# First attention of a two-layer network in a fixed TensorE order, with a different division of the PSUM banks

## The chip, the cores and the metric

The kernel runs on one core of one Trainium2 chip. The metric is the device time of one launch in microseconds (us). Its engines are named as in the profile: PE is TensorE's matmul (PEld its weight load), DVE is VectorE, ACT is ScalarE, POOL is GpSimd, SP is SyncE, which issues the DMAs here. PSUM, into which PE writes, has eight banks of 512 fp32 columns on 128 partitions.

## The reference

Two layers over 1024 latent tokens and 256 context tokens of width 1024. The first has windowed attention with 16 query heads on 4 key/value heads, a sink logit for each head and a rotary embedding; the second has a two-dimensional neighbourhood attention. The change concerns the first. Cut to it:

```python
q, k, v, g = _split_a(u @ w_in)                  # u: modulated tokens
q, k = axial rotary of q and k                   # context: without
s_lat = q_block @ k[3 blocks of 128] * scale     # |i - j| <= 128, masked
s_ctx = q_block @ kc[256] * scale
p = softmax([s_lat, s_ctx, sink])
o = p_lat @ v_block + p_ctx @ vc                 # sink has no value
y = (o * silu(g)) @ w_out
h = layer_norm(alpha * h + gate * y)
```

## The kernel before

Matmuls work in a reduced fp32 format, and operands are split into a high part and the rest (`wh`, `wl`; `uAh`, `uAl`), so that a projection takes three matmuls for each of eight pieces of the inner dimension: high times high, rest times high, high times rest (L208 to L210, tile `pj`).

The attention runs over head pairs p = 0 to 7. A pair has 10 blocks b of 128 queries (8 latent, 2 context) and two heads, so 20 steps k; `S_A43` is the score of step 43, that is p = 2, b = 1, the second head. Blocks 1 to 6 see five tiles of 128 keys, blocks 0 and 7 four, the two context blocks two. One step is:

- `qkA`: the scores on PE (L705, L706; latent and context keys, for the high and the low half of the key: `kA0_0`, `kA0_1`), into `S_A`.
- `sm_first`: DVE reads the scores out of PSUM, adds the mask and takes the extremum (L318); POOL places the sink in a further column (L323); ACT takes the exponential and its sum (L325).
- `sm_second`: DVE's reciprocal (L329), and POOL's product with it (L330).
- `sm_transpose`: PE transposes the probabilities, one matmul for each key tile (L337, into `T_A`); ACT copies them as the high part (L341, `pth`), DVE subtracts that from `T_A` for the rest (L343, `ptl`).
- `pvA_fn`: when both heads of a block are split, PE multiplies the values with the high parts and then with the rests (L734, into `pvA`, one bank for two blocks). After each second block ACT and DVE add its halves (L743, L745) and POOL multiplies with the gate path `gA` (L748).

`att_steps` lays these out as rows, one for each step k: the transposes of k, the scores of k + 3, and one half of the values of an earlier block. `merge` mixes the rows with the fill, which is the projection of this pair's gate path and of the next pair's queries: it hands out fill in proportion to the cost of the attention work done so far. Between them stand small dot products (`dot_half`, L600, L618, L619), for which `gh` is loaded at the first.

What `merge` emits is only a program order. A scheduler then decides each engine's order from priorities, which `lift` raises for some instructions, and from its own estimate of when operands are ready.

PSUM before is one pool: two tiles of two banks under the tag "big", which scores and transposes take in turn, and four banks under the tag "one" for projections (`pj`) and values (`pvA`).

## Time and profile before

| | us |
|---|---|
| median of three runs | 1442.06 (1436.31 to 1512.86) |
| profiled execution | 1437.72 |
| its span | 1435.9 |
| PE busy in the span | 1388.1 |
| DVE busy | 983.6 |
| ACT busy | 732.4 |
| POOL busy | 632.1 |

A row of the profile's groups names the line, the engine, the operation, the tiles written and read, shapes and count, then the busy time in us and the mean of one in ns, and the idle time of that engine ahead of these instructions with the instruction that ended it. A row of the waits has the waiting instruction, the one waited for, the total in us, the number of times and the longest. A row of the timeline starts with the start and the duration in us.

### The profile page before, as it was taken

How to read it: one execution, taken by the hardware profiler on the slowest of the kernel's cores; microseconds unless marked ns; L12 is line 12 of the kernel's file. 1: busy time of each engine (PE TensorE's matmuls, PEld its weight loads, DVE VectorE, ACT ScalarE, POOL GpSimd, SP SyncE). 2: the span in 40 equal slices, each digit the busy share in tenths (PEclk: the TensorE clock that was granted, in tenths of full speed). 3: DMA queues.
4: the chain of work that ended last, by engine and by line, in shares of the span. 5: the costliest groups of instructions: out<-in, count | busy, mean ns of one | idle time of the engine just before them, and what ended most of it. 6: DMA issues, size and time to landing. Idle time of an engine off the chain costs nothing. (4 is left out here: it accounts for less than half of the span.)

```text
span 1435.9 us, 25168 instructions
## 1 busy us (share of the span) xinstructions
PE 1388.1 (97%) x8815; PEld 1214.4 (85%) x8816; DVE 983.6 (68%) x2216; ACT 732.4 (51%) x1561; POOL 632.1 (44%) x779
## 2 busy tenths in 40 slices
PE   8999999999999999999999999999999999998995
PEld 5888898888988888788898899888988899887774
DVE  4658887878888788566433765555565565667798
ACT  4337776676776778332222545554455444557210
POOL 0326766667666666233311333333233323336664
PEclk9999999999999999999999999999999999999998
DMA  9472114123222123434287565555555565374453
GB/s 370 167 237 79 51 63 125 52 78 100 71 71 63 56 84 117 134 129 134 74 257 221 147 187 171 138 162 152 160 150 165 137 180 153 101 206 146 116 135 92
DMA packets 117229, 195.05 MB, mean 136 GB/s; under 512 B 9328, under 2 KB 57840, under 8 KB 117104
## 3 DMA queue, kind: packets, MB, share of 16 engines
q1 hardware_dynamic: 117104, 193.45, 44.5%
q8 instruction: 70, 1.15, 0.3%
q14 instruction: 55, 0.45, 0.1%
HBM read 141.51 MB, written 51.90 MB: 135 GB/s over the span
## 5 line engine op out<-in xcount | busy, mean ns | idle before, releaser
L330 POOL TENSOR_SCALAR s_B<-s_B,rs_B 128x640 f32<-128x640 f32 (+1 forms) x128 | 101.4, 793 | 293.4 <-DVE rs_B L329 264.3
L208 PE MATMUL pj<-uBh,wh 128*128 128x512 f32 (+1 forms) x448 | 175.9, 393 | 0.0
L209 PE MATMUL pj<-uBl,wh 128*128 128x512 f32 (+1 forms) x448 | 170.2, 380 | 0.0
L210 PE MATMUL pj<-uBh,wl 128*128 128x512 f32 (+1 forms) x448 | 170.1, 380 | 0.0
L325 ACT ACTIVATE s_B<-s_B,m_B 128x640 f32<-128x640 f32 (+1 forms) x128 | 102.9, 804 | 129.2 <-DVE m_B L318 129.0
L325 ACT ACTIVATE s_A<-s_A,m_A 128x641 f32<-128x641 f32 (+2 forms) x160 | 119.5, 747 | 83.2 <-DVE m_A L318 64.1
L164 POOL TENSOR_TENSOR wl<-wr,wh 128x512 fp32r<-128x512 f32 x64 | 87.0, 1360 | 160.1 <-ACT wh L162 148.1
L330 POOL TENSOR_SCALAR s_A<-s_A,rs_A 128x640 f32<-128x640 f32 (+2 forms) x160 | 129.3, 808 | 62.4 <-DVE rs_A L329 56.3
L318 DVE CUSTOM_DVE_ANT_0 s_A<-S_A,msk,nsk 128x640 f32<-128x640 f32 (+2 forms) x160 | 123.5, 774 | 32.5 <-PE S_A L706 17.0
L343 DVE TENSOR_TENSOR pt_B<-T_B,pt_B 128x640 fp32r<-128x640 f32 (+1 forms) x128 | 100.9, 788 | 62.8 <-ACT pt_B L341 62.4
L208 PE MATMUL pj<-uAh,wh 128*128 128x512 f32 (+1 forms) x384 | 140.1, 365 | 0.8 <-DVE otmp L745 0.8
L209 PE MATMUL pj<-uAl,wh 128*128 128x512 f32 (+1 forms) x384 | 137.6, 358 | 0.0
L210 PE MATMUL pj<-uAh,wl 128*128 128x512 f32 (+1 forms) x384 | 137.3, 357 | 0.0
L343 DVE TENSOR_TENSOR ptl_A<-T_A,pth_A 128x640 fp32r<-128x640 f32 (+2 forms) x160 | 114.1, 713 | 14.1 <-PE pvA L734 7.0
L337 PE MATMUL T_A<-ident,s_A 128*128 128x128 f32 x672 | 100.8, 274 | 10.5 <-DVE m_A L318 5.5
L337 PEld LDWEIGHTS T_A<-ident,s_A 128*128 128x128 f32 x672 | 77.5, 140 | 36.7 <-issue 10.0
L341 ACT CAST pt_B<-T_B 128x640 fp32r<-128x640 f32 (+1 forms) x128 | 84.3, 659 | 47.3 <-PE T_B L337 46.7
L318 DVE CUSTOM_DVE_ANT_0 s_B<-S_B,bias 128x640 f32<-128x640 f32 (+1 forms) x128 | 100.3, 784 | 10.9 <-PE S_B L1038 10.0
L341 ACT CAST pth_A<-T_A 128x640 fp32r<-128x640 f32 (+2 forms) x160 | 96.3, 602 | 15.8 <-PE T_A L337 14.3
L210 PEld LDWEIGHTS pj<-uBh,wl 128*128 128x128 f32 x448 | 84.3, 188 | 16.6
L337 PE MATMUL T_B<-ident,s_B 128*128 128x128 f32 x608 | 88.1, 274 | 6.9 <-POOL gB L1079 2.7
L209 PEld LDWEIGHTS pj<-uBl,wh 128*128 128x128 f32 x448 | 84.7, 189 | 9.1
(219 smaller groups left out, 3879.8 us busy)
## 6 DMA issues: line engine op xcount, KB each, us to landing
kB<-kdB SPq DMA_DIRECT2D x64, 320.0 KB, 5.3
gw<-in_wadaT SPq DMA_DIRECT2D x48, 256.0 KB, 2.8
vdB<-st SPq DMA_DIRECT2D x20, 512.0 KB, 3.4
vB<-vdB SPq DMA_DIRECT2D x16, 640.0 KB, 4.5
wada<-in_wadaC SPq DMA_DIRECT2D x16, 512.0 KB, 9.6
kdB<-st SPq DMA_DIRECT2D x16, 512.0 KB, 2.8
qdB<-st SPq DMA_DIRECT2D x16, 512.0 KB, 3.5
qB<-qdB SPq DMA_DIRECT2D x32, 256.0 KB, 4.6
```

The costliest lines, as they stand in the source:

```text
L164: e.tensor_tensor(lo, r, f32(hi), ALU.subtract)
L208: mm(pt[:, :n], hi[:, sl], rh, start=kt == 0, stop=False)
L209: mm(pt[:, :n], hi[:, sl], rl, start=False, stop=False)
L210: mm(pt[:, :n], lo[:, sl], rh, start=False, stop=kt == KT - 1)
L318: nc.vector.tensor_tensor_reduce(outp, sc, in1, scale, init if init is not None else 3e38, ALU.add, ALU.min, accum_out=s.m)
L325: nc.scalar.activation(s.t[:, :n], s.t[:, :n], AF.Exp, bias=s.m, scale=-1.0, accum_out=s.sum)
L330: nc.gpsimd.tensor_scalar(s.t[:, : s.w], s.t[:, : s.w], s.rs, 1.0, ALU.mult, ALU.mult)
L337: nc.tensor.transpose(tp[:, k * P : (k + 1) * P], s.t[:, src * P : (src + 1) * P], ident)
L341: nc.scalar.copy(pt.hi[:, :n, hl, :], tv)
L343: nc.vector.tensor_tensor(pt.lo[:, :n, hl, :], tv, f32(pt.hi[:, :n, hl, :]), ALU.subtract)
```

## The change

The order of work up to the start of the first attention, and from the output projection on, stays as it was. In between:

- PSUM is divided anew while the first attention runs (`Banks`, pool "psA"): one tile of two banks for scores, one bank each for the first four transposes of the first and of the second head (`T0`, `T1`), one bank for the fifth transposes of both heads (`T2`), one bank for values, two for projections. After the first block of the output projection the old division comes back.
- `sm_transpose` for the first attention: four transposes into T0 or T1, the fifth into T2, where the second head's lies beside the first's. The first four are split for each head, the fifth tiles of both heads together after the second head. That gives 48 instructions more on ACT and on DVE.
- All PE instructions of pairs 0 to 6 are pinned to the program order (`pin`); those of pair 7 are not.
- `merge` has a lead of 1000 and a burst of 600 there: no more than one piece of fill (three projections) between two steps of attention, and one piece ahead.
- Values of blocks with even b stand in one row, both halves; those of odd b remain apart.
- In pairs 2, 4 and 6 the first three scores come about a row later.
- The instructions behind the values (L743, L745) have a priority raised by 60.

In the new kernel all matmuls have the line L94 and the transposes L367; the split is at L371 and L373.

```diff
+        def one(self, name):
+            if name[0] == "T":
+                return self.ps.tile([P, 512], F32, tag=name[:2], bufs=1, name=name)
+            if self.att:
+                return self.ps.tile([P, 512], F32, tag="pv" if name[:2] == "pv" else "pj", bufs=1 if name[:2] == "pv" else 2, name=name)
+            return self.ps.tile([P, 512], F32, tag="one", bufs=4, name=name)
...
-    def merge(att, fill, lead=0.0):
+    def merge(att, fill, lead=0.0, burst=1e9):
...
-            if jf < len(fill) and (ia == len(att) or jf < need or cf - lead <= ca * (tf - lead) / ta):
+            if jf < len(fill) and (ia == len(att) or jf < need or (run < burst and cf - lead <= ca * (tf - lead) / ta)):
...
+        m = min(n, 4)
+        tp = psone(f"T{hl}_{name}")
+        for k in range(m):
+            transpose(tp[:, k * P : (k + 1) * P], order[k])
+        if n == 5:
+            if hl == 0:
+                pt.fifth = psone(f"T2_{name}")
+            transpose(pt.fifth[:, hl * P : (hl + 1) * P], order[4])
+        split(pt.hi[:, :m, hl, :], pt.lo[:, :m, hl, :], tp[:, : m * P].rearrange("p (k q) -> p k q", k=m))
+        if n == 5 and hl == 1:
+            split(pt.hi[:, 4], pt.lo[:, 4], pt.fifth[:, : 2 * P].rearrange("p (h q) -> p h q", h=2))
...
+            def v_both(k=k):
+                pv(k - 3, 0)
+                pv(k - 3, 1)
...
             if split and 0 <= k - 2 < n and last_of_unit(k - 2):
-                row.append((costs[2] / 2, v_first, 0))
+                if subs[k - 2][1] % 2:
+                    row.append((costs[2] / 2, v_first, 0))
             elif split and k - 3 >= 0 and last_of_unit(k - 3):
-                row.append((costs[2] / 2, v_second, need(k - 3, k + ahead)))
+                if subs[k - 3][1] % 2:
+                    row.append((costs[2] / 2, v_second, need(k - 3, k + ahead)))
+                else:
+                    row.append((costs[2], v_both, need(k - 3, k + ahead)))
...
+    pinned.append(True)
     for p in range(8):
-        att = [x for row in rowsA[p * 20 : (p + 1) * 20] for x in row]
+        rows_p = [list(row) for row in rowsA[p * 20 : (p + 1) * 20]]
+        if p == 7:
+            pinned.clear()
+        elif p % 2 == 0 and p:
+            s = [rows_p[n].pop(1) for n in range(3)]
+            rows_p[1].append(s[0])
+            rows_p[2].insert(1, s[1])
+            rows_p[2].append(s[2])
+        att = [x for row in rows_p for x in row]
...
-            merge(att, gprojA(p) + qprojA(p + 1), lead=0.0)
+            merge(att, gprojA(p) + qprojA(p + 1), lead=1000.0, burst=600.0)
```

Three places of the order. First PE in pair 2, from the transposes of step 43 on. In the names `T_A43` is a tile of transposes, `S_A46` one of scores, `pj18_1` a projection; the last number of each name only counts tiles. Before:

```order
L337 MATMUL T_A43_2910<-ident_63,s_A43_2817 128x128 x5
L208 MATMUL pj18_1_2848<-uAh1_106,wh19_2273 128x512
L705 MATMUL S_A46_2927<-kA1_0_2126,qA4_2426 128x384
L706 MATMUL S_A46_2927<-kA1_0_2126,qA4_2426 128x256
L705 MATMUL S_A46_2927<-kA1_1_2682,qA4_2426 128x384
L706 MATMUL S_A46_2927<-kA1_1_2682,qA4_2426 128x256
L209 MATMUL pj18_1_2848<-uAl1_109,wh19_2273 128x512
L210 MATMUL pj18_1_2848<-uAh1_106,wl19_2274 128x512
L734 MATMUL pvA2_0_2942<-pth_A40_2803,vA1_2167 128x256 x4
```

and after:

```order
L367 MATMUL T1_A43_2963<-ident_63,s_A43_2861 128x128 x4
L367 MATMUL T2_A42_2924<-ident_63,s_A43_2861 128x128
L94 MATMUL S_A46_2973<-kA1_0_2167,qA4_2449 128x384
L94 MATMUL S_A46_2973<-kA1_0_2167,qA4_2449 128x256
L94 MATMUL S_A46_2973<-kA1_1_2722,qA4_2449 128x384
L94 MATMUL S_A46_2973<-kA1_1_2722,qA4_2449 128x256
L94 MATMUL pj18_1_2879<-uAh1_106,wh19_2291 128x512
L94 MATMUL pj18_1_2879<-uAl1_109,wh19_2291 128x512
L94 MATMUL pj18_1_2879<-uAh1_106,wl19_2292 128x512
L367 MATMUL T0_A44_2992<-ident_63,s_A44_2900 128x128 x4
L367 MATMUL T2_A44_2997<-ident_63,s_A44_2900 128x128
```

Before, four value matmuls and six projections stood between the transposes of steps 43 and 44 (the last three projections are behind the quoted rows); after, three projections do, and the fifth tiles of step 42 and of step 44 use the same bank.

Then DVE at the same place (`s_A46` is the read of the score, `rs` the reciprocal, `ptl` the split, `otmp` the sum of the values). Before:

```order
L343 TENSOR_TENSOR ptl_A42_2872<-T_A43_2910,pth_A42_2871 128x5x128
L318 ISA s_A46_2932,m_A46_2933<-S_A46_2927,msk_141,nsk_142 128x640
L318 ISA m_A46_2933 128x1
L329 RECIPROCAL rs_A46_2935<-sum_A46_2934 128x1
L318 ISA s_A47_2967,m_A47_2968<-S_A47_2962,msk_141,nsk_142 128x640
```

and after:

```order
L358 RECIPROCAL rs_A45_2936<-sum_A45_2935 128x1
L347 ISA s_A46_2978,m_A46_2979<-S_A46_2973,msk_141,nsk_142 128x640
L347 ISA m_A46_2979 128x1
L373 TENSOR_TENSOR ptl_A42_2918<-T1_A43_2963,pth_A42_2917 128x4x128
L373 TENSOR_TENSOR ptl_A42_2918<-T2_A42_2924,pth_A42_2917 128x256
L358 RECIPROCAL rs_A46_2981<-sum_A46_2980 128x1
L347 ISA s_A47_3006,m_A47_3007<-S_A47_3001,msk_141,nsk_142 128x640
```

The split of step 43 stood ahead of the read of step 46 and stands behind it now, in two instructions.

Last, PE at the start of the attention. Before, fourteen projections of `pj10_0` stand ahead of the first score; these are the last two of them and what follows:

```order
L208 MATMUL pj10_0_1115<-uAh0_105,wh11_991 128x512
L209 MATMUL pj10_0_1115<-uAl0_108,wh11_991 128x512
L705 MATMUL S_A0_1119<-kA0_0_975,qA0_1030 128x256
L706 MATMUL S_A0_1119<-kA0_0_975,qA0_1030 128x256
L705 MATMUL S_A1_1131<-kA0_0_975,qA1_1031 128x256
L706 MATMUL S_A1_1131<-kA0_0_975,qA1_1031 128x256
L210 MATMUL pj10_0_1115<-uAh0_105,wl11_992 128x512
```

and after, from the first projection of `pj10_0` on:

```order
L94 MATMUL pj10_0_1119<-uAh0_105,wh10_989 128x512
L94 MATMUL pj10_0_1119<-uAl0_108,wh10_989 128x512
L94 MATMUL pj10_0_1119<-uAh0_105,wl10_990 128x512
L94 MATMUL S_A0_1123<-kA0_0_979,qA0_1034 128x256 x2
L94 MATMUL S_A0_1123<-kA0_1_982,qA0_1034 128x256 x2
L94 MATMUL pj10_0_1119<-uAh0_105,wh10_989 128x512
L94 MATMUL pj10_0_1119<-uAl0_108,wh10_989 128x512
L94 MATMUL pj10_0_1119<-uAh0_105,wl10_990 128x512
L94 MATMUL S_A1_1138<-kA0_0_979,qA1_1035 128x256 x2
```

Three projections now stand ahead of the first score, and the score takes both halves of the key in one go. On SP the two loads of `gh` move from behind two weight loads to right behind the load of the values; on DVE the product with `gh` (L661, L612 before) moves ahead of the read of S_A1, and the load of the second key half of pairs 2, 4 and 6 moves ahead of a weight load.

66 lines of the change are left out of this document (46 added, 20 removed).

## The prediction

> **What bounds the kernel now.** I read the page first.
>
> ```profile
> span 1435.9 us, 25168 instructions
> ...
> PE 1388.1 (97%) x8815; PEld 1214.4 (85%) x8816; DVE 983.6 (68%) x2216; ACT 732.4 (51%) x1561; POOL 632.1 (44%) x779
> ```
>
> TensorE (PE) is busy for 97% of the span, so the time is its work plus the moments in which it waits. The change touches only the first attention, about 95 to 575 us. Stretches of 72 us inside it (columns: length, then busy us of PE, weight loads, VectorE, ScalarE and GpSimd, the clock, DMA share, GB/s):
>
> ```profile
> 144.00:216.00 72.00, 69.48 (x464) 62.33 (x464) 61.08 (x151) 51.75 (x120) 50.20 (x71) 1.00 0.17 56
> 216.00:288.00 72.00, 68.65 (x445) 60.04 (x443) 58.06 (x143) 48.96 (x114) 48.06 (x71) 1.00 0.30 89
> 288.00:360.00 72.00, 70.08 (x451) 60.70 (x450) 59.48 (x145) 50.80 (x116) 48.21 (x69) 1.00 0.31 92
> 360.00:432.00 72.00, 70.68 (x478) 63.76 (x477) 59.36 (x145) 52.70 (x122) 49.67 (x70) 1.00 0.21 67
> 432.00:504.00 72.00, 70.73 (x463) 62.23 (x462) 57.74 (x142) 49.33 (x113) 45.76 (x68) 1.00 0.20 61
> ```
>
> Over these 360 us PE is recorded idle for 360 - 349.62 = 10.4 us at a full clock (1.00); VectorE is busy for 295.7 us, 82%. PE leads, and VectorE is a close second. The groups by line and shape, for 100 to 520 us, say where PE idles and give the prices of the next part:
>
> ```profile
> L337 PE MATMUL T_A<-ident,s_A 128*128 128x128 f32 x584 | 87.3, 274 | 8.2 <-DVE m_A L318 3.9 <-POOL s_A L330 2.8 <-POOL s_A L323 0.4
> L318 DVE CUSTOM_DVE_ANT_0 s_A<-S_A,msk,nsk 128x640 f32<-128x640 f32 x84 | 74.0, 881 | 22.9 <-POOL s_A L330 10.7 <-PE S_A L706 10.1 <-POOL s_A L323 1.0
> L706 PE MATMUL S_A<-kA,qA 128*128 128x256 f32 x280 | 73.5, 284 | 2.0 <-DVE ptl_A L343 2.0
> ...
> L343 DVE TENSOR_TENSOR ptl_A<-T_A,pth_A 128x640 fp32r<-128x640 f32 x84 | 68.9, 821 | 7.1 <-ACT pth_A L341 3.9 <-PE pvA L734 1.7 <-issue 0.4
> ...
> L705 PE MATMUL S_A<-kA,qA 128*128 128x384 f32 x168 | 57.2, 363 | 0.5 <-DVE ptl_A L343 0.5
> ...
> L618 DVE CUSTOM_DVE_ANT_0 gj<-gw,gh 128x512 f32<-128x512 f32 x48 | 38.4, 801 | 0.8 <-DMA gw<-in_wadaT 0.4
> ...
> L318 DVE CUSTOM_DVE_ANT_0 s_A<-S_A,msk,nsk 128x512 f32<-128x512 f32 x28 | 20.7, 749 | 5.0 <-PE S_A L706 4.4
> ...
> L343 DVE TENSOR_TENSOR ptl_A<-T_A,pth_A 128x512 fp32r<-128x512 f32 x28 | 19.2, 686 | 0.0
> ...
> L705 PE MATMUL S_A<-kA,qA 128*128 128x256 f32 x56 | 16.9, 325 | 1.6 <-DVE ptl_A L343 1.1 <-DMA kA<-kdA 0.6
> ...
> L318 DVE DVE_READ_ACCUMULATOR2_ANT m_A<- 128x1 f32 x140 | 11.5, 82 | 0.0
> L343 DVE TENSOR_TENSOR ptl_A<-T_A,pth_A 128x256 fp32r<-128x256 f32 x25 | 10.5, 420 | 5.2 <-PE pvA L734 5.1
> ...
> L612 DVE SCALAR_TENSOR_TENSOR gh<-gth,gh 128x512 f32<-128x512 f32 x4 | 3.2, 796 | 0.8 <-ACT gth L611 0.5 <-issue 0.3
> L611 ACT ACTIVATE gth<-gh 128x512 f32<-128x512 f32 x4 | 2.5, 630 | 0.8 <-DMA gh<-in_cr 0.8
> ```
>
> PE's recorded idle time is before transposes (8.2 us) and scores (2.0 + 0.5 + 1.6 = 4.1): 12.3 us, nothing before projections. Scores and transposes share two tiles of two banks, so each kind waits until VectorE has read the other; the waits name just that:
>
> ```profile
> PEld T_A L337 <- POOL s_A L330: 9.4, 16, 1.4
> PE T_A L337 <- DVE m_A L318: 5.5, 8, 1.2
> ...
> PEld S_A L705 <- DVE ptl_A L343: 4.1, 11, 1.3
> ```
>
> The records hide part of each wait. In the timeline a 512-column matmul is 0.39 us long, yet the next starts 0.23 after it:
>
> ```profile
> 102.31 0.28 PE L705 MATMUL S_A<-kA,qA 128*128 128x256 f32 x1
> ...
> 102.67 0.28 PE L706 MATMUL S_A<-kA,qA 128*128 128x256 f32 x1
> ...
> 102.78 0.40 PE L210 MATMUL pj<-uAh,wl 128*128 128x512 f32 x1
> ...
> 103.72 0.34 PE L705 MATMUL S_A<-kA,qA 128*128 128x384 f32 x1
> ...
> 104.18 0.28 PE L706 MATMUL S_A<-kA,qA 128*128 128x256 f32 x1
> ...
> 104.30 0.39 PE L208 MATMUL pj<-uAh,wh 128*128 128x512 f32 x1
> ...
> 104.53 0.39 PE L209 MATMUL pj<-uAl,wh 128*128 128x512 f32 x1
> ```
>
> ```profile
> 386.81 0.71 PE L337 MATMUL T_A<-ident,s_A 128*128 128x128 f32 x5
> ...
> 387.28 0.48 PE L208 MATMUL pj<-uAh,wh 128*128 128x512 f32 x1
> ```
>
> So each wait is up to 0.39 - 0.23 = 0.16 us longer than its idle time. The three wait rows alone hold 16 + 8 + 11 = 35 waits; with an estimate of 45, PE loses 12.3 + 45 x 0.16 = 19.5 us to waits in the seven head pairs. By the distances between starts about 0.6 us a pair (my estimate) is in many small ones that no bank explains, and I leave those 4 us. **At most some 15 us can be won.** Prices from these rows: three projections 3 x 0.23 = 0.69 us; a full score takes PE 104.30 - 103.72 = 0.58 and is complete 104.18 + 0.28 - 103.72 = 0.74 after its start; a short one (256 + 256) takes 102.78 - 102.31 = 0.47 and is complete after 0.64; five transposes 387.28 - 386.81 = 0.47.
>
> **The change part by part.** *Scores and transposes in banks of their own.* The waits of one kind for the other go: -15 us, the amount above. If the order brought new waits of the same kind the gain would be smaller; at nothing gained it is 0.
>
> *One bank for both fifth tiles.* Transposes of five tiles now put the fifth in T2, and VectorE empties it only after the second head, as its own instruction behind the score read. T2 is single: the next pair's first fifth transpose waits. In the order this reads T2_A42, S_A46, projections, T0_A44, T2_A44. From the start of S_A46: its score is complete at 0.74; VectorE reads it (0.881 + 0.082), splits T1_A43 (0.686), then T2_A42 (0.420), to 2.81. PE arrives at T2_A44 at 0.58 + 0.69 + 4/5 of 0.47 = 1.65. **It waits 1.16 us.** For the block pair around T2_A48, three projections stand ahead of S_A50 and the split of T1 is done earlier: 0.69 + 0.74 + 0.96 + 0.42 = 2.81 against 0.69 + 0.58 + 0.69 + 0.38 = 2.34, 0.47 us. For T2_A52 the score is short and no projection follows it: 0.69 + 0.64 + 0.83 + 0.42 = 2.58 against 0.69 + 0.47 + 0.38 = 1.54, 1.04 us. For odd blocks a row of values or more stands between, and nothing waits. Sum 2.67 us a pair, and since the order of later pairs is the same, 7 x 2.67 = 18.7 us. If VectorE comes late to the score read (it is busy 82%), up to about 1 us a pair is added; nothing can make it less but a PE that is already late. I take 18.7 and add 2 for lateness, with 17 to 26 as bounds. Here a wait queues everything: S_A47 and all the fill stand behind it on PE.
>
> The Trainium skill (Perfetto Trace Analysis, Matmuls) says that independent matmul groups should rotate through different PSUM banks so that the evacuation of one overlaps the matmuls of the next; by that alone the change would win its 15 us. The same page (Optimization Strategy) says that the same gap repeating can mean that too little PSUM is there for the next tile, which is what a single T2 would show, and by it the sum is the one that I make. No run here has shown T2 yet.
>
> *The two splits more.* VectorE replaces two reads of 640 by two of 512 and one of 256: 2 x (686 - 821) + 420 = +150 ns for each of six pairs of blocks, 0.9 us a head pair, beside PE work; ScalarE does the like. I cost it at nothing beyond T2's chain: VectorE has 18% left. Without that cover it is 7 x 0.9 = 6 us.
>
> *The start.* Before, fourteen projections (from 95.19) stand ahead of the first score; pinned, it is three. Timeline and DMA issues (for 88 to 110 us, the last column is us to landing; then the tile kA over the whole run):
>
> ```profile
> 91.98 2.58 SPq L679 DMA_DIRECT2D kA<-kdA  x4
> ...
> 94.73 0.46 SPq L684 DMA_DIRECT2D vA<-vdA  x1
> ...
> 95.19 0.40 PE L208 MATMUL pj<-uAh,wh 128*128 128x512 f32 x1
> ...
> 98.97 0.91 SPq L609 DMA_DIRECT2D gh<-in_cr  x2
> ```
>
> ```profile
> kA<-kdA SPq DMA_DIRECT2D x6, 320.0 KB, 6.3
> ...
> vA<-vdA SPq DMA_DIRECT2D x1, 640.0 KB, 8.0
> ...
> gh<-in_cr SPq DMA_DIRECT2D x2, 256.0 KB, 5.9
> ```
>
> ```profile
> DMA to landing us min/median/max: 3.9/5.6/8.0
> ```
>
> PE reaches S_A0 at 95.19 + 0.69 = 95.88. Its second half needs the fourth kA load, issued near 93.9, landing near 100.2: PE waits about 4.1 us there (1.7 to 5.8 by the ends 3.9 and 8.0). Before, projections hid this. S_A1 waits for the read of S_A0: 0.3. Then gh: its two loads are now issued right behind vA, near 95.2, and VectorE's product with them stands before the read of S_A1, for which S_A2 waits. By 5.9 us they land at 101.1, by vA's 8.0 at 103.2; I take a value near vA's, the load right ahead in the same queue. From 103.2: tanh 0.63, product 0.80, read 0.83, so 105.5; PE arrives near 102.6, and waits 2.9, or 0.8 by the earlier landing. I take 2.4. Together **6.8 us** (2 to 9).
>
> *Pairs 2, 4, 6.* Their first three scores come a row later, and the second key half is loaded ahead of the weight load that it stood behind. The order leaves about 7 us of PE work between load and use: 5.6 us is hidden, 8.0 is not, 0.7 to 1 each; with a late first transpose I take 2 us for the three (0 to 4).
>
> *No cost:* the one bank of values (its next use is over a row behind the reads that free it), two of projections (a group is 24 matmuls, 5.5 us, behind which the evacuation of the other one lies), values of even blocks in one row (they are read a row later than they are ready). If one of these covers went, a pair would lose some tenths for each group. The last pair is not pinned, and at the hand-over the second gate waits for a copy out of the shared scores tile: 0.5 us. The fill of one piece between steps moves work and adds none.
>
> Sum: -15 + 18.7 + 2 + 6.8 + 2 + 0.5 = **+15 us**. The profiled execution took 1437.72 us (1.8 around its span), the median of the three runs is 1442.06, 4 us above it; against the former the forecast is 1453 us.
>
> **The rivals.**
> *A, the gain holds.* Separate banks take nearly all of 19.5 us and T2 is cheap, since PE is late for another reason when it gets there, and the loads land early (start 2 us): 1437.7 - 19.5 + 2 + some 4 = 1424 us. For it: the waits for the other kind are real. Against: T2's chain consists of rows in a fixed order and PE's work between is counted. Chance 0.12.
>
> *B, about even.* The pinned order is so near to that before that stalls move places: T2 at its low end and the start at 2 us, 1437.7 - 15 + 17 + 2 - 2 = 1440. Chance 0.18. It is also the case in which the change does nothing to speak of.
>
> *C, VectorE becomes the pace.* With a fixed order, PE can't take projections while VectorE is late. VectorE's 82% plus 0.9 us a pair is near 84% of a row's time; where a fill instruction such as the 801 ns product or a rotation stands ahead of a read, each score and split behind it is late and PE pays at once. At 0.3 us for each of 140 rows, 42 us: 1480. It decides against the forecast from an average of 0.1 us a row upward beyond what I counted. For it: 82%, and VectorE's waits for scores (10.1 us on the 640 reads), which show the two in lock step. Against: before, too, VectorE takes its instructions in one order, and the small waits come to 0.6 us a pair. Chance 0.16.
>
> **How the numbers follow.** Forecast case 0.54, at 1453, with 1440 to 1466 from its own bounds (T2 -2 to +5, start -5 to +2, pairs 2, 4 and 6 -2 to +2, gain 12 to 19). A 0.12 at 1424; B 0.18 at 1440; C 0.16 at 1480 (1465 to 1500). The range of 8 in 10 reaches from 1432 (A left out but for its upper edge) to 1472 (the lower part of C): outside lie 0.10 and 0.10. This kernel's runs differ by some per cent, so about 2% (29 us, 1409 and 1466) is what can be told from no change. Faster by more: 0.02, the outermost of A. Slower by more: 0.16, most of C and the edge of the forecast. Same: 0.82.
>
> **What would show it.** In the changed profile: a repeated wait of PE on T2 for ptl_A, three times a pair, 1.1, 0.5 and 1.0 us; hardly any wait of T0, T1 or S for the other kind; PE idle for about 4 us near 96 to 100 us, waiting for DMA of kA, and 2 to 3 us before the third score, by way of gh; from 600 us on nothing but a shift. It is wrong if T2 isn't among PE's waits, if the gap at the start is under 2 us, or if waits stand in all rows rather than in three of ten blocks, which is C.

## The result and the profile after

The change makes the kernel slower: 1491.86 us (median of four runs) against 1440.87. One run of each kernel was slow (1713.88 and 1512.86 us); without these two the ratio is 1.0364, with a 95% interval of 1.0349 to 1.0379. The profiled execution took 1492.0 us. The forecast was 1453 us in a range of 1432 to 1472: the sign was right, the size was wrong by a factor of about 3.5.

First the page, then stretches of the first attention (columns as before: length, busy us of PE, weight loads, VectorE, ScalarE, GpSimd, clock, DMA share, GB/s). The second row is the five stretches of before in one.

```profile
span 1490.2 us, 25208 instructions
...
PE 1398.1 (94%) x8816; PEld 1224.2 (82%) x8816; DVE 985.5 (66%) x2264; ACT 735.5 (49%) x1609; POOL 625.0 (42%) x779
```

```profile
96.00:108.00 12.00, 8.24 (x35) 6.14 (x34) 9.13 (x17) 6.11 (x13) 4.68 (x6) 0.72 1.08 269
144.00:504.00 360.00, 326.57 (x2130) 289.89 (x2129) 280.13 (x711) 237.73 (x575) 219.46 (x324) 1.00 0.23 68
```

PE is recorded idle for 360 - 326.57 = 33.4 us from 144 to 504 us, where it was 10.4. VectorE is less busy there (280.13 us) than before (295.7): it did not become the bound by load. From 96 to 108 us the mean granted clock is 0.72. Now PE's waits:

```profile
PE T_A L367 <- DVE ptl_A L373: 29.1, 22, 1.9
...
PE S_A L94 <- DVE m_A L347: 12.9, 17, 1.6
...
PE yA L94 <- DVE z L983: 8.3, 1, 8.3
...
PE gate L417 <- ACT gates L418: 2.0, 1, 2.0
PE S_A L94 <- DMA kA<-kdA: 1.8, 1, 1.8
PE pj L94 <- DVE st L292: 1.5, 1, 1.5
```

The first row is the fifth tiles' bank T2, 22 waits, three in each pinned pair and one in the last. In the second row a score waits for the read of the score before it. The third is one wait of 8.3 us at the hand-over to the output projection. The prediction had the first with a smaller sum (20.7 us with its 2 for lateness), of the second only what it expected at the start (0.3 us, and 2.4 by way of gh), and the third not at all.

Where the 54.3 us between the two profiled executions lie, by the start of the first score read of each pair and of the first transposes behind the output projection:

| stretch | before | after | more |
|---|---|---|---|
| start to the first score read | 102.7 | 103.4 | 0.7 |
| pairs 0 to 6 | 418.6 | 454.3 | 35.7 |
| last pair and hand-over | 74.0 | 87.7 | 13.7 |
| from there to the end | 840.6 | 844.8 | 4.2 |

The rows come out of these starts, of VectorE's first read in the first and in the last pair and of PE's first transposes of the output block, before:

```profile
102.75 0.75 DVE L318 CUSTOM_DVE_ANT_0 s_A<-S_A,msk,nsk 128x512 f32<-128x512 f32 x1 [2.46 <-PE S_A L706]
...
521.32 0.75 DVE L318 CUSTOM_DVE_ANT_0 s_A<-S_A,msk,nsk 128x512 f32<-128x512 f32 x1
...
595.32 1.09 PE L871 MATMUL uT<-ident,z 128*128 128x128 f32 x8 [1.67 <-ACT z L917]
```

and after:

```profile
103.40 0.75 DVE L347 CUSTOM_DVE_ANT_0 s_A<-S_A,msk,nsk 128x512 f32<-128x512 f32 x1
...
557.66 0.75 DVE L347 CUSTOM_DVE_ANT_0 s_A<-S_A,msk,nsk 128x512 f32<-128x512 f32 x1
...
645.39 1.03 PE L943 MATMUL uT<-ident,z 128*128 128x128 f32 x8
```

One wait on T2 in the timeline, that of T2_A48 in pair 2:

```profile
264.80 0.75 PE L94 MATMUL S_A<-kA,qA 128*128 128x384 f32 x4
...
265.26 0.85 DVE L797 TENSOR_TENSOR otmp<-pvA,otmp 64x256 f32<-64x256 f32 x2 [0.50 <-ACT otmp L795]
...
266.08 0.60 PE L367 MATMUL T_A<-ident,s_A 128*128 128x128 f32 x4
266.14 0.69 DVE L373 TENSOR_TENSOR ptl_A<-T_A,pth_A 128x512 fp32r<-128x512 f32 x1
...
266.75 0.88 DVE L347 CUSTOM_DVE_ANT_0 s_A<-S_A,msk,nsk 128x640 f32<-128x640 f32 x1
...
267.55 0.42 DVE L373 TENSOR_TENSOR ptl_A<-T_A,pth_A 128x256 fp32r<-128x256 f32 x1
...
268.12 0.30 PE L367 MATMUL T_A<-ident,s_A 128*128 128x128 f32 x1 [1.44 <-DVE ptl_A L373]
```

The score is complete near 264.80 + 0.74 = 265.54, but VectorE reads it only from 266.75: the sum of the values (otmp, 0.85) and the first split (0.69) stand ahead. That is 1.2 us that the prediction's chain did not hold.

And the hand-over:

```profile
619.50 1.59 PE L417 MATMUL gate<-ident,dcol 128*128 128x128 f32 x8 [1.96 <-ACT gates L418]
...
630.70 1.28 DVE L983 SCALAR_TENSOR_TENSOR z<-z,yA 128x512 f32<-128x512 f32 x2 [3.37 <-DMA z<-in_htok]
...
632.04 0.80 PE L94 MATMUL yA<-woAh,og 128*128 128x512 f32 x1 [8.34 <-DVE z L983]
632.63 0.63 PE L94 MATMUL yA<-woAl,og 128*128 128x512 f32 x1
633.06 1.06 PE L94 MATMUL yA<-woAh,og 128*128 128x512 f32 x2
```

The second block of the output projection is put into the two projection banks in which the first block's result still stands. VectorE empties them when the residual z has come by DMA, at 630.70, and until 632.04 PE has nothing. Before, the second block had other banks, and PE worked on it while VectorE waited for the same load:

```profile
590.24 1.29 DVE L911 SCALAR_TENSOR_TENSOR z<-z,yA 128x512 f32<-128x512 f32 x2 [3.40 <-DMA z<-in_htok]
590.29 0.39 PE L422 MATMUL yA<-woAh,og 128*128 128x512 f32 x1
```

After, the matmuls behind the gap start 0.43 us apart (632.63, 633.06) in place of 0.23: the granted clock is at 0.50 from 619.9 to 637.0 us.

### The profile page after: what moved, and what is told of

Same layout as the page of the kernel before. It is cut to its first block, busy times and chain, and to the rows that moved or that the text cites. A ratio compares the mean times of both kernels' runs of the same rounds, so it can differ in the third digit from the quotient of the medians.

```text
span 1490.2 us, 25208 instructions
## 1 busy us (share of the span) xinstructions
PE 1398.1 (94%) x8816; PEld 1224.2 (82%) x8816; DVE 985.5 (66%) x2264; ACT 735.5 (49%) x1609; POOL 625.0 (42%) x779
## 5 line engine op out<-in xcount | busy, mean ns | idle before, releaser
L359 POOL TENSOR_SCALAR s_B<-s_B,rs_B 128x640 f32<-128x640 f32 (+1 forms) x128 | 101.8, 796 | 294.0 <-DVE rs_B L358 263.9
L94 PE MATMUL pj<-uBh,wh 128*128 128x512 f32 (+1 forms) x448 | 175.8, 392 | 0.0
L94 PE MATMUL pj<-uBl,wh 128*128 128x512 f32 (+1 forms) x448 | 170.2, 380 | 0.0
L94 PE MATMUL pj<-uBh,wl 128*128 128x512 f32 (+1 forms) x448 | 170.0, 380 | 0.0
L359 POOL TENSOR_SCALAR s_A<-s_A,rs_A 128x640 f32<-128x640 f32 (+2 forms) x160 | 125.6, 786 | 80.3 <-DVE rs_A L358 77.4
L189 POOL TENSOR_TENSOR wl<-wr,wh 128x512 fp32r<-128x512 f32 x64 | 84.0, 1313 | 172.7 <-ACT wh L187 164.7
L94 PE MATMUL pj<-uAh,wh 128*128 128x512 f32 (+1 forms) x384 | 146.1, 380 | 2.3 <-DVE st L292 1.5
L373 DVE TENSOR_TENSOR pt_B<-T_B,pt_B 128x640 fp32r<-128x640 f32 (+1 forms) x128 | 101.0, 789 | 63.9 <-ACT pt_B L371 63.4
L94 PE MATMUL pj<-uAl,wh 128*128 128x512 f32 (+1 forms) x384 | 137.3, 358 | 0.0
L94 PE MATMUL pj<-uAh,wl 128*128 128x512 f32 (+1 forms) x384 | 137.3, 358 | 0.0
L367 PE MATMUL T_A<-ident,s_A 128*128 128x128 f32 x672 | 105.2, 275 | 32.7 <-DVE ptl_A L373 29.1
L94 PE MATMUL S_A<-kA,qA 128*128 128x384 f32 (+1 forms) x576 | 114.2, 316 | 15.0 <-DVE m_A L347 12.9
L367 PEld LDWEIGHTS T_A<-ident,s_A 128*128 128x128 f32 x672 | 81.5, 140 | 52.0 <-issue 25.0
L373 DVE TENSOR_TENSOR ptl_A<-T_A,pth_A 128x512 fp32r<-128x512 f32 (+1 forms) x208 | 117.8, 583 | 9.5 <-ACT pth_A L371 8.3
L94 PEld LDWEIGHTS S_A<-kA,qA 128*128 128x128 f32 x576 | 90.2, 192 | 30.5 <-DVE m_A L347 21.5
L94 PE MATMUL yA<-woAh,og 128*128 128x512 f32 x320 | 103.6, 400 | 8.5 <-DVE z L983 8.3
L371 ACT CAST pt_B<-T_B 128x640 fp32r<-128x640 f32 (+1 forms) x128 | 84.4, 659 | 48.8 <-PE T_B L367 48.3
L371 ACT CAST pth_A<-T_A 128x512 fp32r<-128x512 f32 (+1 forms) x208 | 98.9, 501 | 12.9 <-PE T_A L367 9.5
```

Source lines behind the costliest of these rows:

```text
L94: pin(nc.tensor.matmul(*a, **kw))
L189: e.tensor_tensor(lo, r, f32(hi), ALU.subtract)
L359: nc.gpsimd.tensor_scalar(s.t[:, : s.w], s.t[:, : s.w], s.rs, 1.0, ALU.mult, ALU.mult)
L367: pin(nc.tensor.transpose(out, s.t[:, src * P : (src + 1) * P], ident))
L371: nc.scalar.copy(hi, src)
L373: nc.vector.tensor_tensor(lo, src, f32(hi), ALU.subtract)
```

## The experiments

All but the last are one run each; the kernel before took 1438.0 to 1441.0 us beside them (seven runs of it spread over 3.8 us), so that a difference of two or three microseconds between two of them says little. Waits are as recorded, without the 0.16 us that the prediction adds for each. "Pairs" are the lengths from first read to first read, as in the table above.

**1. T2 freed without VectorE.** The rest of the fifth tiles is computed from the high part in SBUF, which makes it zero: this kernel leaves out the low part of the fifth tiles and keeps an instruction of the same size.

```diff
-                nc.vector.tensor_tensor(lo, src, f32(hi), ALU.subtract)
+                nc.vector.tensor_tensor(lo, src if psum else f32(hi), f32(hi), ALU.subtract)
...
-            split(pt.hi[:, 4], pt.lo[:, 4], pt.fifth[...])
+            split(pt.hi[:, 4], pt.lo[:, 4], pt.fifth[...], False)
```

> The rests of the fifth tiles are worked out from the high part in SBUF and not from T2 in PSUM (so the rests of the fifth tiles are zero, and the output a little less exact); VectorE keeps an instruction of the same size at the same place, but T2 is now free as soon as ScalarE has copied it. Theory 1 (T2's release by VectorE costs three waits of 1.1 to 2.0 us in each of seven pairs, about 31 us): PE's waits on T2 go to about 0.3 us or less and the time falls by 22 to 31 us, to 1461 to 1470. Theory 2 (VectorE is the pace, and any wait taken away comes back at the next score or transpose): the waits move to S_A and T, the time falls by less than 10 us, above 1482.

1474.84 us, 17 less; the waits of this run:

```profile
PEld S_A L94 <- DVE m_A L347: 34.1, 42, 2.3
PE S_A L94 <- DVE m_A L347: 21.9, 31, 2.0
```

No transpose waits for VectorE's split any more, so all 29.1 us of that row are gone; but scores wait 21.9 us for the read of the score before (12.9 in the change). About a third of what T2 cost comes back one step later. Neither theory has it alone: T2 is a real wait, and right behind it stands the single scores tile. Of the 17 us, 4.6 lie behind the attention (840.2 us to the end, not 844.8), where the edit changes nothing; the last section says where a part of such differences comes from.

**2. Other places for the banks.** Dummy tiles fix the order in which the new pool places its banks.

```diff
     banks.open("psA", True)
+    banks.big("spareS")
+    banks.one("T0_spare")
+    banks.one("T1_spare")
+    banks.one("T2_spare")
```

> Only the places of the banks in the new pool are changed: scores first, then T0, T1, T2, then projections and values. By this the first projections no longer stand in the bank that the last value projections leave, and the output projection's second block starts in the bank of the scores, not in those of the first block. Theory 1 (the two changes of pool are paid by PE: 1.65 + 0.9 us near 89 and 98 us, and 8.6 us behind the first output block with a stretch at half clock, 12 us in all): 1492 falls to 1477 to 1481. Theory 2 (the gap at the hand-over is due to the load of the residual, which VectorE awaits at 630 us): PE waits there all the same, the time falls by no more than 4 us.

1482.20 us, 9.7 less. The last pair and hand-over take 79.2 us in place of 87.7, which is 8.5 of the 9.7, and the 8.3 us wait is gone: PE starts the second output block at 624.14. So it was the place of the banks; the load of z was not what PE had to wait for. At the start nothing was won: the wait at 89 us (1.5) went, but projections then waited 2.2 us for the rotation to read the group two before (0.8 in the change); there are two banks for them where there were four.

**3. Pair 0 not pinned.**

```diff
-    pinned.append(True)
     for p in range(8):
+        if p == 1:
+            pinned.append(True)
```

> PE instructions of the first head pair are not pinned, those of pairs 1 to 6 are. Theory 1 (the pinned start lets PE wait for the keys and for the product with gh, and the gap halves the clock): the start loses 2 us in place of 8, and no half clock shows from 100 to 108 us: the time falls by 6 to 10 us, to 1482 to 1486. Theory 2 (the start costs little, since what PE does not wait there it waits for later in the pair): within 3 us of 1492.

1484.69 us, 7.2 less, but not as theory 1 has it: PE still waits for the keys (2.4 us), the clock is still halved from 101.0 us on, and pair 0 wins 3.0 us (64.6 in place of 67.6), its T2 waits of 4.9 us replaced in part by others. 3.1 us of the gain lie behind the attention, so that the pinned start itself is worth some 4 us.

**4. Nothing pinned.**

```diff
-    pinned.append(True)
```

> Nothing is pinned; banks, fill and the order of the program stay those of the change. Theory 1 (single banks, T2 above all, cause the loss, and a scheduler can only hide a part of it by moving projections before the waiting transposes): T2 waits shrink to a half, the time falls by 15 to 30 us, to 1462 to 1477. Theory 2 (the pinned order is the cause, since it takes PE the choice of other work): about 1440, the time of before. Theory 3 (the banks alone): 1487 or more.

1464.42 us, 27.4 less, in theory 1's range and far from 1440. T2 nearly stops being waited for:

```profile
L367 PE MATMUL T_A<-ident,s_A 128*128 128x128 f32 x626 | 97.2, 273 | 3.5 <-POOL s_A L359 1.9 <-DVE rs_A L358 1.1 <-DVE ptl_A L373 0.5
```

This group is all transposes from 100 to 560 us; in the change its idle time is 29.4 us. The scheduler had put work between T0 and T2. Between the first four transposes of step 44 and the fifth there now stand three projections, the next score and a value matmul, where the pinned order has nothing:

```
T0_A44, 2 x pj, 4 x S_A47, 1 x pj, pvA, T2_A44
T0_A48, 2 x pj, 2 x S_A51, T2_A48
T0_A52, 3 x pj, 2 x S_A55, T2_A52
```

**5. The old banks, pinned.** Five transposes in one tile, one split; scores and transposes in turn, as before; order, fill and rows of the change.

```diff
-        if not a:
+        if True:
             tp = psbig(f"T_{name}")
...
-    banks.st.close()
-    banks.open("psA", True)
...
-        if b == 0:
-            banks.st.close()
-            banks.open("psB")
```

> The pinned order, the even fill and the rows of the change, but the banks of before (scores and transposes take turns in two tiles of two banks, five transposes in one tile and one split of all five; four banks for projections and values). Theory 1 (the pinned order of short rows is the cause, since a split must be read in the time of one score and three projections, whatever the bank): PE waits at transposes about as often, and only the hand-over and the opening of the pool get well: 1470 to 1480. Theory 2 (the single T2 is the cause): 1440 to 1455.

1495.84 us, above theory 1's range and 40 us above theory 2's. Here there is no T2, and PE waits as much:

```profile
PE T_A L367 <- DVE m_A L347: 24.1, 28, 1.8
...
PE S_A L94 <- DVE ptl_A L373: 9.7, 11, 1.6
PE T_A L367 <- DVE ptl_A L373: 6.5, 11, 0.9
```

The hand-over is well (last pair and hand-over 77.4 us) but pairs 0 to 6 take 469.0 us, 14.7 more than with the new banks. **In this pinned order the new banks win some 15 us in the pairs; so it is not they that lose there.** The form of the wait depends on the banks, the wait does not.

**6. Values of even blocks in two rows again.**

```diff
-                if subs[k - 2][1] % 2:
-                    row.append((costs[2] / 2, v_first, 0))
+                row.append((costs[2] / 2, v_first, 0))
```

(and `v_second` likewise)

> The values of even blocks stand in two rows again, as before the change; pinned, banks of the change. This puts five value matmuls (0.6 us) between the score and the fifth transpose at all three places of a pair, and three projections more at the last. Theory 1 (T2 waits because its row is short): the waits on T2 fall by 0.6, 0.6 and 1.0 to 1.2 us, some 15 us in all, to 1475 to 1480. Theory 2 (VectorE is the pace over a whole pair, so that work moved between rows gives nothing): 1488 to 1496.

1474.27 us, 17.6 less. The waits on T2 fall from 29.1 to 7.9 us, by more than forecast; but the time does not follow it all the way (pairs 0 to 6 win 13.7 us, and 2.9 lie behind the attention), for PE now waits for the single bank of values, which it did not inside the pinned pairs of the change:

```profile
PE pvA L94 <- DVE otmp L797: 10.8, 12, 1.7
...
PE T_A L367 <- DVE ptl_A L373: 7.9, 16, 0.8
```

One row for both halves and a short row beside it are two sides of one choice: it spares the bank of values and makes PE wait for T2.

**7. The first three scores of pairs 2, 4, 6 at their old place.**

```diff
-        elif p % 2 == 0 and p:
+        elif False:
```

> Only the delay of the first three scores of pairs 2, 4 and 6 is undone. Theory 1 (three scores in two rows wait for each other's read, 1.75 and 0.5 us, and the transposes behind them 0.5 us): these waits go, 2 to 2.5 us for each of three pairs, 6 to 8 us, to 1484 to 1486. Theory 2 (the delay covers the load of the keys, and without it PE waits for the DMA as long): 1490 to 1494.

1489.44 us, 2.4 less, between the theories. The waits at the three pairs' starts go (6.5 us in all), and 1.2 to 1.5 us of waiting for the keys' DMA come at each of the three places, with 0.2 for a read (4.1 us in all): just the 2.4 us of difference. The delay does cover a load, at a higher price than the load.

**8. The banks alone.** Experiment 2's places, nothing pinned; fill, rows, scores and priority as before the change.

```diff
-    pinned.append(True)
...
-LIFT_PV = 60
+LIFT_PV = 0
...
-            merge(att, gprojA(p) + qprojA(p + 1), lead=1000.0, burst=600.0)
+            merge(att, gprojA(p) + qprojA(p + 1), lead=0.0)
```

> The banks of the change (with the places of the second experiment) and the split of the fifth tiles, but nothing pinned, and fill, rows, scores and priorities as before. Theory 1 (the single banks cost little where the scheduler is free): the unpinned run less 10 us for the places and less 3 to 8 us for the rest, 1446 to 1452. Theory 2 (single banks cost as such, VectorE's added splits too): 1460 or more. Theory 3 (more overlap of scores and transposes): below 1438.

1448.40 us, as theory 1 has it: 10 us above the kernel before, not below it.

```profile
144.00:504.00 360.00, 347.84 (x2272) 307.53 (x2271) 295.88 (x753) 251.41 (x609) 245.92 (x343) 1.00 0.24 73
```

Inside the attention PE idles 12.2 us of 360, about as before (10.4). PE's largest wait is for the single bank of values (otmp, 10.8 us in 11 times); scores and transposes hardly wait for one another.

**9. The banks alone, pinned.** Against experiment 8:

```diff
+    pinned.append(True)
```

> The run with the banks alone (1448), and pairs 0 to 6 pinned to their program order, which here is that of the old fill, rows and scores. Theory 1 (pinning as such costs, since the program order leaves short rows, whatever the fill): 25 to 45 us more, 1473 to 1493. Theory 2 (only the change's own fill and rows make the pinned order bad): within 8 us of 1448.

1522.41 us, 74 more than without the pin: more than either theory allowed. The waits are of yet other kinds:

```profile
PE pvA L94 <- DVE otmp L801: 51.4, 26, 2.8
...
PE S_A L94 <- DMA kA<-kdA: 14.8, 4, 5.1
```

The program order of the old kernel was never meant to be PE's order. The change's rows, fill, delays and priority repair it by 1522 - 1482 = 40 us (against experiment 2, which has the same places), and the rest stays.

**10. As 8, pool opened later, transposes placed first, priority 60.**

```diff
     merge([], qprojA(0))
+    banks.st.close()
+    banks.open("psA", True)
+    banks.one("T0_spare")
+    banks.one("T1_spare")
+    banks.one("T2_spare")
+    banks.one("pv_spare")
```

> The run with the banks alone (1448), with the new pool opened only after the first pair's query projections, transposes and values placed first, and the raised priority (60) behind the values, which that run lacked. Theory 1 (what the banks alone cost is the opening of the pool, 2.8 us near 98 us, and the single bank of values, 2.5 to 3 us in each odd pair): the wait at 98 us goes, that on otmp falls to a half, 1440 to 1444. Theory 2 (single banks cost as such): 1446 or more.

1455.57 us, 7 more than experiment 8: theory 1 falls. The wait on the rotation went as expected (the first score read is at 101.8, not 103.1), but the waits on otmp stayed at some 2.5 us in odd pairs (2.6 to 3.1 in run 8), and the last pair and hand-over take 77.7 us in place of 75.0. Which of the three edits costs this is not told apart here.

**11. As 10, values of even blocks in one row.**

```diff
-                row.append((costs[2] / 2, v_first, 0))
+                if subs[k - 2][1] % 2:
+                    row.append((costs[2] / 2, v_first, 0))
```

> As the run before, and the values of even blocks in one row as in the change. Theory 1 (one row for both halves leaves the single bank of values a row more, so that the wait on otmp goes altogether): 1436 to 1441. Theory 2 (the rows next to it get short, and scores wait for their read): 1442 to 1450, with waits of S_A on the read in odd pairs.

1451.07 us. Odd pairs get shorter (61.6 us on average, 65.4 in run 10), even ones longer (59.6, from 58.4), and scores wait for their read. The waits on otmp do go in the odd pairs, as theory 1 has it; the time is theory 2's, a microsecond above its range.

**12. Experiments 2, 3 and 6 together.**

```diff
+    banks.big("spareS")
...
+        if p == 1:
+            pinned.append(True)
...
-                if subs[k - 2][1] % 2:
```

(with the new lines of 2 and 6 as there)

> Pinned, fill and scores of the change, with three parts undone together: other bank places, pair 0 free, values of even blocks in two rows. Theory 1 (these losses lie in different places and add up: 9.7 + 7.2 + 17.6 us by their own runs): 1454 to 1461. Theory 2 (each wait that goes uncovers another): 1465 or more.

1467.37 us: 24.5 less, where 34.5 would be the sum. The number is theory 2's, its reason is not: by stretches the gains do add up where they were made, 15.4 us in pairs 0 to 6 (16.6 by the three runs) and 8.8 in the last pair and hand-over (9.1). Of the 10 us that lack, 7.4 lie behind the attention (844.4 us, in place of 841.7 to 843.1 in the three runs), where none of the edits changes the work, and 1.3 at the start.

**13. Priority of the instructions behind the values at 0.**

```diff
-LIFT_PV = 60
+LIFT_PV = 0
```

> Only the raised priority of the instructions behind the values (60) is set back to 0; pinned, all else as in the change. Theory 1 (the raised priority makes the last, free pair end its attention early and leaves output work that nothing covers): the last pair gets longer and the hand-over shorter, 3 to 6 us less in all, 1486 to 1489. Theory 2 (with the order pinned it decides nothing): within 2 us of 1492.

1501.28 us, 9.4 *more*: both theories fall. The pairs get longer, since PE then waits for the bank of values (otmp, 15.0 us in 7 times):

```profile
PE T_A L367 <- DVE ptl_A L373: 27.4, 21, 2.3
...
PE pvA L94 <- DVE otmp L797: 15.0, 7, 3.0
```

The priority moves VectorE's instructions, which PE's pinned order then awaits; so "with the order pinned it decides nothing" was wrong. The lateness seen at 265.26 us above is not its price: with priority 0 the sum of the values stands ahead of the same split and read (268.84 us), and the same transpose waits 1.44 us as well.

**14. Only the projections free.** Scores, transposes and values stay pinned.

```diff
-                    mm(pt[:, :n], hi[:, sl], rh, start=kt == 0, stop=False)
+                    nc.tensor.matmul(pt[:, :n], hi[:, sl], rh, start=kt == 0, stop=False)
```

(and the two matmuls behind it likewise)

> Scores, transposes and values stay pinned among themselves; only the projections are free, so that the scheduler may place them before a transpose that would wait. Theory 1 (pinning costs because PE cannot take fill while a split is read): most of the 27 us that the unpinned run won is won here too, 1464 to 1474. Theory 2 (the order of scores, transposes and values among each other costs): 1484 or more.

1467.76 us, 24.1 of the 27.5 us that came of pinning nothing. T2's waits fall to a quarter:

```profile
144.00:504.00 360.00, 342.18 (x2231) 301.73 (x2231) 295.91 (x739) 247.64 (x600) 232.94 (x338) 1.00 0.24 72
```

```profile
PE T_A L367 <- DVE ptl_A L373: 6.9, 16, 1.0
```

Idle time from 144 to 504 us goes from 33.4 to 17.8. This is the run that settles the larger part of the pairs' share. Pairs 0 to 6 take 433.9 us: 20.4 of the 35.7 us come back with the projections alone free, and only 2.6 more with nothing pinned (experiment 4). The attention's own order costs little; what costs is that three projections are nailed to each step while PE waits with others ready to run. Of the 12.7 us that stay with nothing pinned, 7.9 are there in experiment 8 too, which has the old fill, rows, scores and priority: 5.3 of these lie in pair 0.

**15. As 10, priority 0, both halves in one row in odd pairs alone.**

```diff
-LIFT_PV = 60
+LIFT_PV = 0
...
-                row.append((costs[2] / 2, v_first, 0))
+                if subs[k - 2][1] % 2 or subs[k - 2][0] % 2 == 0:
+                    row.append((costs[2] / 2, v_first, 0))
```

> The banks of the change, nothing pinned, old fill and scores, the pool opened late with transposes first, priority 0, and both halves of even blocks in one row in the odd pairs alone, where the run before showed them to help (61.6 against 63.7 us a pair), not in the even ones (59.5 against 56.2). Theory 1 (the parts add up: the banks alone, 1448, less 2 us for each of three odd pairs and 1 to 3 us at the start): 1438 to 1442, level with the kernel before. Theory 2 (what one pair gains, its neighbour gives back): 1446 or more.

1448.11 us, the median of four runs: ratio 1.0057, interval 1.0038 to 1.0077. Theory 2: against experiment 8 the odd pairs keep 1 to 1.5 us each, and the last pair with the hand-over loses 2.7. Pairs 1 to 6 take 361.5 us (before: 362.5; the banks alone, in experiment 8: 365.1); so with a free order the new banks are worth at best 1 us over six pairs, and that with the rows of odd pairs fitted to them. The 11 us by which the profiled execution is longer lie elsewhere: first read 0.8 later, pair 0 4.3 longer, last pair and hand-over 3.7 longer, and 3.2 behind the attention. No run here beat the kernel before.

## Why the prediction was wrong

Term by term, the forecast against what the profile and the runs showed:

| term | forecast, us | shown |
|---|---|---|
| waits of scores and transposes for each other | -15 | gone; in their place 5.9 us of scores waiting for the read of the score before (the other 7.0 of the 12.9 are in the rows "start" and "pairs 2, 4, 6") |
| T2 | +20.7 | 28.2 us recorded in the pinned pairs, 31.5 with 0.16 for each of 21 waits |
| start | +6.8 | 2.3 (pool) + 1.8 (keys) + 1.2 (score reads), and a stretch at half clock |
| pairs 2, 4, 6 | +2 | 6.5 in all, 5.8 of it scores waiting for reads |
| hand-over | +0.5 | with the last pair +13.7 |
| behind it | 0 | +4.2 |

The sum fell short by 54.3 - 15 = 39 us. With 0.16 us for each wait, the hand-over was 13 us over its forecast, T2 11, scores waiting for their own reads in the rows and in pairs 2, 4 and 6 another 13, and what lies behind the attention 4. That is 41 us, an estimate, with the gain of 15 left as it was; so the steps that failed are the waits that the new single tiles bring, and the hand-over.

*The step on the banks of their own.* "The waits of one kind for the other go: -15 us" was right in its words and wrong as a sum. S_A has a single tile, and in a pinned row with three projections the next score arrives at 1.65 + 0.1 = 1.75 us, when the read of the one before ends at 0.74 + 0.96 = 1.70: 0.05 us to spare, so that PE pays for any lateness of VectorE. I had both numbers in the chain for T2 and did not carry them on to S_A47, which stands right behind. Experiment 1 shows it bare: with T2 free, 21.9 us stand there. Nor were the 15 us all waits of one kind for the other: the largest of the three rows that I gave for them, 9.4 us, waits for GpSimd's product, which is what the transposes read, and of the 12.3 us recorded only 7.5 (3.9 + 2.0 + 0.5 + 1.1) end with VectorE's read or split. (The 3.2 us of waiting for GpSimd fall to 0.7 in the change as well; no run says why.) A wait taken away has to be followed to the next instruction in the queue.

*The step on T2* had the right mechanism, place and count (three a pair), and was mis-sized: 1.16, 0.47 and 1.04 us were forecast; 1.38, 1.44 and 0.95 are recorded in pair 2, which is 1.54, 1.60 and 1.11 with the 0.16 us that a record hides. The third holds, the first is short by 0.4 and the second by 1.1 us, for VectorE's sum of the values, awaiting ScalarE, stands in its order ahead of the first split and the read. I took the order behind the read from the list, and not what stands ahead of it. The 21 waits come to 31.5 us where the chain had 18.7, and the second of each three makes 8.7 of the 12.8 us between; so my 2 us "for lateness" should have been some 13.

*The step "No cost"* on projections said that two banks are enough, looking only at gates and projections inside the attention. The tiles yA0 of the output projection take the same two banks, and the next pool puts the second output block on top of them. Before, that block filled the very gap in which VectorE waits for z. Experiment 2 gave 9.7 us back by places alone, 8.5 of it in this stretch, for which I had 0.5; and those were meant for the gate's wait for its copy, recorded with 2.0.

*The start* came out near its size by another sum. The load of the keys cost 1.8, not 4.1: the opening of the new pool, which I had not costed, had already made PE 2.3 us late. The product with gh cost 0.8 where I took 2.4. The half clock was not in the sum.

*Rival C* came nearest in size (42 us), the right cause "with a fixed order, PE can't take projections while VectorE is late", and a wrong reading of VectorE: it is no fuller than before (280.13 us of 360, where it was 295.7). It is latency in a fixed order, not load. I gave it 0.16 for its load; its first sentence deserved more, and experiments 4, 5 and 14 bear that sentence out. *Rival A*, the gain by banks, found no support: with the order free, pairs 1 to 6 are 2.6 us longer than before with the banks alone (experiment 8) and 1 us shorter with fitted rows (experiment 15). The rule of the Trainium skill that stood for it (Perfetto Trace Analysis, Matmuls) is that independent groups should rotate through different PSUM banks. Here scores, fifth tiles and values each got a single tile, so that the next group of a kind finds no other bank. The other rule of that page (Optimization Strategy, consistent bubbles) is what the trace shows: the same three gaps in each pair.

What stays open: which of its three edits made run 10 slower than run 8; what makes the last pair and hand-over 5.2 us longer than before in experiment 2 too, and pair 0 4 to 5 us longer in experiments 8 and 15; and how much of the +4.2 us behind the attention would repeat in other executions. The change's fill and rows with the old banks and nothing pinned were not run, so their share is known only together with that of the banks.

## What to carry to other kernels

Pinning one engine to the order of the program takes away the scheduler's one means against latency, moving independent work in front of a wait; before doing so, work out for each short row whether every release that the next row needs has come, and let at least the filler float (here 24 of 27 us). A buffer with a single copy is as good as the longest chain that frees it, and when it is freed the next single buffer in the queue becomes the wait. When a pool is divided anew, look at what stands in the old banks at both ends, for the first user of a new bank waits for the last reader of the old one.

## What the runs showed of the hardware

The granted clock halves in short, thin stretches, and it changes at fixed moments. In the changed kernel it falls at 101.11, 497.06, 619.94, 1374.28 and 1480.10 us; the last four lie 116, 152, 373 and 404 times 3.413 us after the first; in the other 16 traces, too, all changes within one lie whole multiples of 3.413 us apart. These are the fixed stretches around the first fall (columns as above):

```profile
97.70:101.11 3.41, 1.22 (x6) 0.86 (x5) 2.40 (x2) 0.25 (x1) 2.50 (x2) 1.00 1.04 211
101.11:104.53 3.42, 2.27 (x6) 1.51 (x7) 2.55 (x5) 2.35 (x5) 1.30 (x2) 0.50 1.17 341
104.53:107.94 3.41, 2.99 (x10) 2.17 (x11) 2.54 (x6) 2.65 (x7) 0.82 (x3) 0.50 1.05 274
```

No wait in them is longer than 1.8 us, yet the clock falls to 0.50 behind the first, in which PE was busy for 1.22 us, and matmuls then start 0.43 us apart. In experiment 14 the thin time at the same place, with a wait of 2.0 us in it, is spread over several of its fixed stretches, and the clock stays at 1.00:

```profile
96.61:100.03 3.42, 1.88 (x11) 1.37 (x10) 2.66 (x3) 0.00 (x0) 2.50 (x2) 1.00 1.01 216
100.03:103.44 3.41, 1.86 (x8) 1.28 (x8) 2.63 (x5) 2.22 (x4) 0.71 (x1) 1.00 1.16 305
```

Counted over the 17 traces, PE was recorded busy for at most 54% of the fixed stretch ahead of each of the 79 halvings, and of the 7064 stretches at full clock that no halving followed the emptiest was at 41%. So it is the filling of a fixed stretch that goes with the halving, and not the length of a single wait. The Trainium skill (TensorE: Matmul & The Clock Gate, What's actually happening) has a free-running window of about 3.4 us that must be idle; the first part agrees with these traces, the second does not, for the stretch ahead of 101.11 us was busy for 36%.

It also tells where a part of the 4.2 us behind the attention comes from, where both kernels have the same instructions in the same order. Near the end of the second attention a transpose waits for GpSimd, 2.13 us before the change and 3.08 after. That wait and the fixed stretches that it touches, before:

```profile
1319.69 0.74 PE L337 MATMUL T_B<-ident,s_B 128*128 128x128 f32 x5 [2.13 <-POOL gB L1079]
```

```profile
1315.61:1319.03 3.42, 1.95 (x16) 1.75 (x14) 2.83 (x4) 1.03 (x3) 2.46 (x3) 1.00 0.38 114
1319.03:1322.44 3.41, 1.94 (x12) 1.57 (x12) 1.30 (x4) 2.78 (x6) 2.72 (x3) 1.00 0.59 226
```

and after:

```profile
1372.33 0.74 PE L367 MATMUL T_B<-ident,s_B 128*128 128x128 f32 x5 [3.08 <-POOL gB L1154]
```

```profile
1370.87:1374.28 3.41, 1.43 (x9) 1.26 (x10) 2.00 (x5) 2.01 (x4) 2.11 (x3) 1.00 0.65 233
1374.28:1377.70 3.42, 3.00 (x12) 2.40 (x12) 2.16 (x6) 2.50 (x6) 2.60 (x3) 0.50 0.03 7
```

Before, the clock stayed at 1.00; after, it was halved for two stretches. The lag behind the kernel before grows there from 51.7 to 54.9 us, of which the longer wait is 0.95 and the rest comes while the clock is halved. It did not take the longer wait: in experiment 7 the wait is 2.12 us, as before the change, but falls nearly whole into one stretch, and the clock is halved as well:

```profile
1369.65 0.74 PE L367 MATMUL T_B<-ident,s_B 128*128 128x128 f32 x5 [2.12 <-POOL gB L1154]
```

```profile
1368.26:1371.67 3.41, 1.45 (x10) 1.28 (x11) 1.94 (x5) 1.85 (x4) 1.99 (x2) 1.00 0.68 234
1371.67:1375.09 3.42, 2.77 (x11) 2.18 (x10) 2.17 (x6) 2.66 (x6) 2.55 (x3) 0.50 0.02 6
```

So where the fixed moments fall can decide over some microseconds. From the first output transposes to the end, the five runs that are halved there for two stretches, the change among them, take 843.9 to 844.9 us, the five that are halved for one 841.5 to 842.0, and the seven that are not, the kernel before among them, 836.6 to 843.4: it is not the whole of the difference. Gains of that size behind the attention, as the 3.1 us in experiment 3 and the 4.6 in experiment 1, are to be read with it.
